# Row vectors through DRAM in 16-byte pieces, read on the chip through strided views

## The chip, the cores and the metric

The kernel runs on one core of one Trainium2 chip, as one launch. The time is the device time of an execution in microseconds (us). All inputs, weights and the output are in DRAM; the profile times are those of one execution.

## The reference

Two transformer blocks over 512 tokens of 1024 numbers, in float32. In the first block a layer that mixes the tokens with a gated MLP (gmlp) is followed by a feed-forward layer (FF), then a layer of sparse attention (nsa) by another FF; the second block is one layer of two kinds of attention side by side. Between the layers stand the operations that matter here; `c` is one vector that steers the whole:

```
def modulate(h, shift, scale):
    return h * (1.0 + scale[:, None, :]) + shift[:, None, :]
...
    mod = c_act @ ada_w[layer] + ada_b[layer]
    sh1, sc1, g1, sh2, sc2, g2 = jnp.split(mod, 6, axis=-1)
    h = modulate(rms_norm(x, norm_g[layer, 0]), sh1, sc1)
...
    x = x + g1[:, None, :] * rms_norm(y, norm_g[layer, 1])
    h = modulate(rms_norm(x, norm_g[layer, 2]), sh2, sc2)
    y = jnp.square(jax.nn.relu(h @ ff_w_in[layer])) @ ff_w_out[layer]
    x = x + g2[:, None, :] * rms_norm(y, norm_g[layer, 3])
```

The second block ends with `x + gate * (mixed @ w_out)`. So each layer needs row vectors of 1024 numbers: a gain G for what it gives out (norm weight times gate), and a scale B and a shift S for the next layer's input.

## The kernel before

The 512 tokens are four chunks (c = 0 to 3) of 128, with tokens in the partitions and the 1024 features along the free axis, in two halves (n = 0, 1) of 512. The stream x stays on the chip (`xs`) until it is set aside in DRAM (`xd`). A float32 product is made of three products of rounded parts, high by high, high by low and low by high; names that end in h and l are such parts (`wh`, `wl` of a weight tile `raw`; `twh`, `twl`, `tah`, `tal` for the last part of an output product), and `fmps` and `acc` are PSUM banks that gather products.

Nothing is issued where it is written: a recorder takes down every operation, plans an order for each engine from a table of its own costs and from the buffers that are free, and then emits the whole (line 615, so nearly every instruction of the profile bears L615 and is found by its tiles). Each engine then goes through its own list in that order and waits where an operand is missing. SP issues all DMAs, in one list. `flex` leaves it to the planner whether DVE or POOL makes a multiplication, `mac` likewise (a product by a scalar per partition, plus a tile). The planner's costs know the number of elements, not their step.

The row vectors come out as columns: `vec` (line 927) takes products of a weight row block with the steering vector on DVE, and leaves a tile [128, 8], where partition p and column k hold element k·128 + p. `col` waits for it and adds the bias. `wide` (line 948) makes rows of it that every partition holds: SP stores the tile to a DRAM scratch row of 1024 numbers, and then reads each half back with a broadcast into a 128x512 tile. This is done for 11 vectors: G1, B2, S2 at the boundary behind gmlp (boundary 1), G2 behind the first FF (2), G3, B4, S4 behind nsa (3), G5, B6, S6 behind the second FF (4), and the gate at the end; a name with w at its end (G1w) is the row. At boundary 2 B and S stay columns (`h_chunk2`). The vectors that `setup` needs at the program's beginning don't go through `wide`.

When a chunk of an output product is done, `boundary` runs three steps for it. `residual` (line 1030): z = acc × G for both halves (DVE), the square sums (ScalarE, named ACT in the profile), 1/rms as `yr`, then x = z·yr + x. `x_rstd`: 1/rms of the new x as `xr`. `h_chunk` (line 1000): hx = x × B (`flex`), hx = hx·xr + S (`mac`), then four transposes of 128x128 for each half on TensorE (PE) into the bank `tp`, from which the next layer's input is split into its parts. `fin` (in `second`) makes the output: fy = acc × gate, fy = fy + x, and the store.

Of the kernel before, what the change touches and what calls it, by code (L numbers as in the profile page):

```python
# [670 lines left out]
class KB:  # L671
# [276 lines left out]
    def wide(self, vec, name):  # L948

        v = self.col(vec)  # L950
        r = self.scratch([1, 1024], name)
        self.sp.dma_start(r.rearrange("o (k p) -> p (o k)", p=128), v)
        t = [self.t2([128, 512], F32, name) for _ in range(2)]
        for n in range(2):
            self.sp.dma_start(t[n], r[:, n * 512:n * 512 + 512].bcast())
        return t


    def x_rstd(self, c):
# [40 lines left out]
    def h_chunk(self, c, r, B, S, hT, keep=None):  # L1000
        if keep is not None:
            return self.h_chunk2(c, r, B, S, hT, keep)
        for n in range(2):
            s = slice(n * 512, n * 512 + 512)
            t = self.t2([128, 512], F32, "hx")
            self.flex("tensor_mul", t, self.xs[c][:, s], B[n])
            self.mac(t, t, r, S[n])
            ps = self.ps("tp")
            for j in range(4):
                self.pe.transpose(ps[:, j * 128:(j + 1) * 128], t[:, j * 128:(j + 1) * 128], self.ident)  # L1010
            cs = slice(c * 128, c * 128 + 128)
            self.split(hT.hi[n][:, :, cs], hT.lo[n][:, :, cs], ps.rearrange("p (j t) -> p j t", j=4))
# [17 lines left out]
    def residual(self, c, banks, G):  # L1030

        ss = self.st(2, "ys")
        z = []
        for n in range(2):
            s = slice(n * 512, n * 512 + 512)
            junk = self.t2([128, 512], F32, "junk")
            self.act.activation(junk, banks[n], AF.Square, accum_out=ss[:, n:n + 1])
            z.append(self.t2([128, 512], F32, "z"))
            self.dve.tensor_mul(z[n], banks[n], G[n])
        r = self.rstd_of(ss, "yr")  # L1040
        for n in range(2):
            s = slice(n * 512, n * 512 + 512)
            x = self.xs[c][:, s]
            self.mac(x, z[n], r, x)
# [631 lines left out]
    def second(self, hT, grow):  # L1676
# [298 lines left out]
        gate = self.wide(grow, "gatew")  # L1975

        def fin(c, banks):
            for n in range(2):
                s = slice(n * 512, n * 512 + 512)
                xt = self.t2([128, 512], F32, "fx")  # L1980
                self.sp.dma_start(xt, self.xd[c][:, s])
                y = self.t2([128, 512], F32, "fy")
                parts = 2 if c == NC - 1 and n == 1 else 1
                for i in range(parts):
                    h = slice(i * 512 // parts, (i + 1) * 512 // parts)
                    self.dve.tensor_mul(y[:, h], banks[n][:, h], gate[n][:, h])
                    self.dve.tensor_add(y[:, h], y[:, h], xt[:, h])
                    self.sp.dma_start(self.out[0, c * 128:(c + 1) * 128, n * 512 + h.start:n * 512 + h.stop], y[:, h])

        self.out_gemm(self.act_f32(mixed), I["w_out_2"][0], KD, fin, CTAIL, split=True)  # L1990

    def build(self):
# [83 lines left out]
```

## Time and profile before

| | |
|---|---|
| median of 3 runs | 1545.78 us (1544.43 to 1546.18) |
| the profiled execution, its own time | 1546.29 us |
| its span | 1544.5 us |
| its mean granted TensorE clock | 0.993 |
| PE busy | 1496.9 us (97%) |
| DVE busy | 1088.8 us (70%) |
| ScalarE busy | 657.2 us (43%) |
| POOL busy | 294.0 us (19%) |
| instructions | 20161 |

Busy time counts an engine's own instructions, not its waiting. In a group of instructions, "idle before" is the time that the engine stood still ahead of them, and behind the arrow stands what ended it. A window is a stretch of the span, in which the busy time of each engine is summed up; a timeline lists one engine's instructions in order of time, with the idle time ahead of one in brackets. In the stages' windows boundary 1 lies at 145 to 205 us, boundary 2 at 495 to 550, boundary 3 at 850 to 905, boundary 4 at 1195 to 1260.

### The profile page before, as it was taken

Reading aid. Unit: us, or ns where it says so; the run is one execution under the profiler, and the core shown is the slowest. Engines: PE = TensorE matmul, PEld = TensorE weight load, DVE = VectorE, ACT = ScalarE, POOL = GpSimd, SP = SyncE. Lnnn points to the kernel's source line nnn. Section 1 sums busy time; section 2 is a strip of 40 time slices with the busy share of each in tenths; the row PEclk is TensorE's granted clock in tenths of the full one; section 3 lists DMA queues with packets and bytes.
Section 4 is the critical chain, followed back from the end, with each engine's and each line's share of the span. In section 5 each row is a group of like instructions: output and inputs, shape, how many; then the busy total and the mean of one; then the engine's idle time right before and its main releaser. Section 6 shows DMA issues by size and latency. Waiting matters only on the chain.

```text
span 1544.5 us, 20161 instructions
## 1 busy us (share of the span) xinstructions
PE 1496.9 (97%) x7410; PEld 1248.8 (81%) x7410; DVE 1088.8 (70%) x2038; ACT 657.2 (43%) x1422; POOL 294.0 (19%) x355
## 2 busy tenths in 40 slices
PE   5999999999999999999999999999999999999998
PEld 4877788888888898778877898888888887878877
DVE  7897866568871679687886864456662669598982
ACT  5523432232120656578774332222120337566870
POOL 2023100000010320465762000000000014132250
PEclk9999999999999999999989999999999999999999
DMA  9874677549620343102124447438411251113112
GB/s 345 263 264 110 213 234 249 171 156 383 271 84 13 133 151 117 52 1 56 28 69 137 135 117 256 134 135 255 154 43 54 96 181 55 55 52 91 50 54 96
DMA packets 151394, 212.97 MB, mean 138 GB/s; under 512 B 49536, under 2 KB 110208, under 8 KB 151296
## 3 DMA queue, kind: packets, MB, share of 16 engines
q1 hardware_dynamic: 151296, 211.69, 42.3%
q8 instruction: 58, 0.95, 0.3%
q14 instruction: 40, 0.33, 0.1%
HBM read 205.33 MB, written 6.34 MB: 137 GB/s over the span
## 4 chain that ended last, share of the span: by engine, by line
PE 76%; DVE 8%; ACT 3%; issue 2%; POOL 1%; DMA 0%; POOLq 0%; DVEq 0%; ACTq 0%
PE acc L615 30%; PE fmps L615 25%; PE qps L615 4%; PE tmc L615 4%; PE po L615 2%; PE sgps L615 2%; DVE wl L615 2%; DVE ptl L615 2%; PE vps L615 1%; PE tmb L615 1%; PE kps L615 1%; PE sB L615 1%; PE tp L615 1%; PE sA L615 1%; PE tA L615 1%
## 5 line engine op out<-in xcount | busy, mean ns | idle before, releaser
L615 DVE TENSOR_TENSOR wl<-raw,wh 128x1024 fp32r<-128x1024 f32 x194 | 240.4, 1242 | 41.3 <-PE fmps L615 18.5
L615 PE MATMUL acc<-wh,ah 128*128 128x512 f32 x432 | 168.9, 391 | 0.0
L615 PE MATMUL acc<-wl,ah 128*128 128x512 f32 x432 | 168.6, 390 | 0.0
L615 DVE CAST wh<-raw 128x1024 fp32r<-128x1024 f32 x118 | 82.9, 703 | 119.9 <-PE fmps L615 93.7
L615 DVE SCALAR_TENSOR_TENSOR raw<-raw,cb 128x1024 f32<-128x1024 f32 x112 | 137.1, 1248 | 11.7 <-DMA raw<-in_kv_ada_w_dram 7.9
L615 PE MATMUL acc<-wh,al 128*128 128x512 f32 x432 | 133.8, 390 | 0.0
L615 ACT ACTIVATE r<-fmps 128x512 f32<-128x512 f32 x64 | 38.2, 597 | 206.9 <-PE fmps L615 206.9
L615 PE MATMUL fmps<-hfh,wl 128*128 128x512 f32 (+1 forms) x288 | 105.5, 366 | 1.1 <-DVE wl L615 1.1
L615 PE MATMUL acc<-twh,tah 128*128 128x512 f32 x272 | 105.1, 392 | 1.1 <-ACT tah L615 1.1
L615 PE MATMUL acc<-twl,tah 128*128 128x512 f32 x272 | 105.4, 393 | 0.6 <-DVE twl L615 0.5
L615 PE MATMUL fmps<-hfl,wh 128*128 128x512 f32 (+1 forms) x288 | 105.2, 366 | 0.2 <-DVE hfl L615 0.2
L615 PE MATMUL fmps<-hf1l,wh 128*128 128x512 f32 (+1 forms) x288 | 105.2, 366 | 0.0
L615 PE MATMUL fmps<-hf1h,wl 128*128 128x512 f32 (+1 forms) x288 | 105.2, 366 | 0.0
L615 PE MATMUL fmps<-hfh,wh 128*128 128x512 f32 (+1 forms) x288 | 105.0, 366 | 0.0
L615 PE MATMUL fmps<-hf1h,wh 128*128 128x512 f32 (+1 forms) x288 | 104.8, 365 | 0.0
L615 ACT CAST ah<-hid 128x512 fp32r<-128x512 f32 x48 | 29.7, 619 | 159.4 <-PE acc L615 159.4
L615 PEld LDWEIGHTS acc<-wh,ah 128*128 128x128 f32 x432 | 81.5, 189 | 16.9
L615 POOL TENSOR_SCALAR tah<-hid 128x512 fp32r<-128x512 f32 x5 | 5.5, 1112 | 470.4 <-DMA raw<-in_ff_w_out_dram 206.5
L615 PEld LDWEIGHTS acc<-wl,ah 128*128 128x128 f32 x432 | 81.4, 188 | 16.8
L615 PEld LDWEIGHTS acc<-wh,al 128*128 128x128 f32 x432 | 81.3, 188 | 16.7
L615 PE MATMUL acc<-twh,tal 128*128 128x512 f32 x272 | 86.8, 394 | 1.1 <-DVE tal L615 1.1
L615 ACT CAST wh<-raw 128x1024 fp32r<-128x1024 f32 x57 | 59.8, 1050 | 55.3 <-PE fmps L615 32.0
(543 smaller groups left out, 3851.4 us busy)
## 6 DMA issues: line engine op xcount, KB each, us to landing
raw<-in_ada_w_dram SPq DMA_DIRECT2D x40, 1024.0 KB, 7.8
raw<-in_ff_w_in_dram SPq DMA_DIRECT2D x32, 1024.0 KB, 9.4
raw<-in_ff_w_out_dram SPq DMA_DIRECT2D x32, 1024.0 KB, 5.0
raw<-in_w_in_dram SPq DMA_DIRECT2D x16, 1024.0 KB, 5.6
raw<-in_w_ada_dram SPq DMA_DIRECT2D x12, 1024.0 KB, 10.8
raw<-in_a_w_in_dram SPq DMA_DIRECT2D x8, 1024.0 KB, 8.9
raw<-in_ada_w_dram SPq DMA_DIRECT2D x16, 512.0 KB, 11.8
raw<-in_kv_ada_w_dram SPq DMA_DIRECT2D x8, 1024.0 KB, 14.2
```

Source lines behind the costliest of these rows:

```text
L615: getattr(real[e], m)(*a, **k)
```

## The change

The store of a row vector writes four neighbouring numbers at a time: of each half n, partition p writes its four columns k behind each other. The half then lies in DRAM, and after the broadcast in the 128x512 tile, in the order p·4 + k, while the feature is k·128 + p. `wide` gives out views of the tiles that read it in the order of the features, [128, 4, 128] with a step of four numbers (16 bytes) in the innermost axis; the users write their other operands in the same three axes (`by4`), which leaves these contiguous. So one operand of each of these multiplications is read with a step, and none is written with one.

```
@@ wide
-        self.sp.dma_start(r.rearrange("o (k p) -> p (o k)", p=128), v)
+        self.sp.dma_start(r.rearrange("o (n p k) -> p (o n) k", n=2, p=128), v.rearrange("p (n k) -> p n k", n=2))
         t = [self.t2([128, 512], F32, name) for _ in range(2)]
         for n in range(2):
             self.sp.dma_start(t[n], r[:, n * 512:n * 512 + 512].bcast())
-        return t
+        return [x.rearrange("q (p k) -> q k p", k=4) for x in t]
+
+    @staticmethod
+    def by4(x):
+
+        return x.rearrange("q (k p) -> q k p", k=4)
@@ h_chunk
-            self.flex("tensor_mul", t, self.xs[c][:, s], B[n])
-            self.mac(t, t, r, S[n])
+            self.flex("tensor_mul", self.by4(t), self.by4(self.xs[c][:, s]), B[n])
+            self.mac(self.by4(t), self.by4(t), r, S[n])
@@ residual
-            self.dve.tensor_mul(z[n], banks[n], G[n])
+            self.dve.tensor_mul(self.by4(z[n]), self.by4(banks[n]), G[n])
@@ fin
-                    self.dve.tensor_mul(y[:, h], banks[n][:, h], gate[n][:, h])
+                    hk = slice(h.start // 128, h.stop // 128)
+                    self.dve.tensor_mul(self.by4(y)[:, hk], self.by4(banks[n])[:, hk], gate[n][:, hk])
```

No instruction changes its place on PE, DVE, ScalarE or POOL. In SP's list, behind the loads for the end of gmlp (`raw<-in_a_w_out_dram`), the stores of G1 and B2 stand where they stood, ahead of a load of the output weight:

```order
 L615 DMA raw<-in_a_w_out_dram 128x2x1024
-L615 DMA G1w<-G_520 128x8x1
-L615 DMA B2w<-B_876 128x8x1
+L615 DMA G1w<-G_520 128x2x4
+L615 DMA B2w<-B_876 128x2x4
 L615 DMA raw<-in_a_w_out_dram 128x2x1024
 L615 DMA G1w<-G1w 128x512 x2
 L615 DMA B2w<-B2w 128x512 x2
```

Only the shape of the two stores is another; the nine stores further on change in the same way. On PE, with the engines that an instruction waits for, the first transposes of a chunk at boundary 1 read:

```order
 L615 MATMUL acc<-twl,tah 128x512
-L615 MATMUL tp<-ident,hx 128x128 [waits DVE_49]
+L615 MATMUL tp<-ident,hx 128x128 [waits DVE_49,Activation_49]
 L615 MATMUL tp<-ident,hx 128x128 x3
 L615 MATMUL acc<-twh,tal 128x512
```

The order is the same, and the first transpose names an event of ScalarE beside that of DVE.

## Rows read from the trace of the kernel before

**Rows 1.** Windows by stage: the four boundaries; us busy by engine, clock, DMA share, GB/s.

```profile
145.00:205.00 60.00, 57.59 (x349) 50.37 (x348) 51.78 (x97) 26.69 (x60) 4.15 (x3) 1.00 0.64 202
...
495.00:550.00 55.00, 55.00 (x261) 45.62 (x260) 33.52 (x86) 32.37 (x83) 16.26 (x25) 1.00 0.46 155
...
850.00:905.00 55.00, 55.00 (x347) 49.64 (x346) 44.46 (x87) 21.90 (x55) 1.72 (x1) 1.00 0.52 173
...
1195.00:1260.00 65.00, 65.00 (x304) 53.73 (x303) 44.99 (x95) 23.54 (x56) 2.94 (x4) 1.00 0.48 164
```

**Rows 2.** DMA issues of the whole program: count, KB each, median us to landing.

```profile
G1w<-G SPq DMA_DIRECT2D x1, 4.0 KB, 10.5
...
xd<-x SPq DMA_DIRECT2D x8, 512.0 KB, 2.6
```

**Rows 3.** Windows around the stores of G1 and B2 and after them.

```profile
116.00:118.00 2.00, 2.00 (x16) 1.81 (x14) 1.26 (x4) 0.60 (x1) 0.00 (x0) 1.00 1.11 5
...
122.00:124.00 2.00, 2.00 (x20) 2.00 (x20) 0.00 (x0) 0.18 (x1) 1.28 (x1) 1.00 0.61 33
...
128.00:144.00 16.00, 13.24 (x53) 9.13 (x52) 15.97 (x16) 6.57 (x9) 10.33 (x6) 1.00 0.51 199
```

**Rows 4.** Timeline of ScalarE: start, us, operation, idle time before it and its releaser.

```profile
123.82 2.00 ACT L615 CAST twh<-raw 128x1024 fp32r<-128x1024 f32 x2 [6.00 <-DMA raw<-in_a_w_out_dram]
```

**Rows 5.** Groups by shape: busy us, mean ns of one, idle before and its releaser.

```profile
L615 DVE SCALAR_TENSOR_TENSOR E<-wsum,lngb,bs 128x128 f32<-128x128 f32 x8 | 2.5, 343 | 0.0
...
L615 DVE SCALAR_TENSOR_TENSOR hx<-hx,xr,S2w 128x512 f32<-128x512 f32 x8 | 5.7, 748 | 1.1 <-DMA S2w<-S2w 1.0
...
L615 DVE SCALAR_TENSOR_TENSOR bl<-R,pos,bh 128x124 fp32r<-128x124 f32 x32 | 13.2, 428 | 1.0 <-ACT bh L615 0.8
...
L615 ACT ACTIVATE PB<-PB,mx 128x128 f32<-128x128 f32 x32 | 12.8, 400 | 5.4 <-DVE mx L615 5.2
...
L615 ACT ACTIVATE PB<-PB,mx 128x384 f32<-128x384 f32 x32 | 19.7, 616 | 4.8 <-DVE mx L615 4.8
...
L615 ACT ACTIVATE bh<-R,pos 128x124 fp32r<-128x124 f32 x32 | 14.3, 509 | 4.2 <-DVE R L615 4.2
...
L615 DVE TENSOR_TENSOR z<-acc,G1w 128x512 f32<-128x512 f32 x8 | 5.4, 685 | 2.4 <-PE acc L615 2.4
...
L615 DVE TENSOR_TENSOR fy<-acc,gatew 128x256 f32<-128x256 f32 x2 | 0.8, 418 | 1.3 <-PE acc L615 1.3
```

**Rows 6.** Timeline of boundary 3, second chunk, DVE then PE.

```profile
863.09 1.29 DVE L615 TENSOR_TENSOR z<-acc,G3w 128x512 f32<-128x512 f32 x2 [0.38 <-PE acc L615]
...
870.54 1.42 DVE L615 SCALAR_TENSOR_TENSOR hx<-hx,xr,S4w 128x512 f32<-128x512 f32 x2
...
872.19 1.29 DVE L615 TENSOR_TENSOR z<-acc,G3w 128x512 f32<-128x512 f32 x2 [0.23 <-PE acc L615]
...
872.67 0.60 PE L615 MATMUL tp<-ident,hx 128*128 128x128 f32 x4
```

**Rows 7.** Timeline of boundary 4, second chunk, DVE then PE.

```profile
1211.68 1.29 DVE L615 TENSOR_TENSOR z<-acc,G5w 128x512 f32<-128x512 f32 x2 [1.86 <-PE acc L615]
...
1217.99 1.41 DVE L615 SCALAR_TENSOR_TENSOR hx<-hx,xr,S6w 128x512 f32<-128x512 f32 x2
...
1220.31 0.60 PE L615 MATMUL tp<-ident,hx 128*128 128x128 f32 x4
```

**Rows 8.** Timeline of boundary 1, last chunk: DVE, POOL, PE.

```profile
177.91 2.36 DVE L615 TENSOR_TENSOR wl<-raw,wh 128x1024 fp32r<-128x1024 f32 x2 [1.38 <-ACT wh L615]
...
185.44 2.04 POOL L615 TENSOR_TENSOR hx<-x,B2w 128x512 f32<-128x512 f32 x1 [1.43 <-DVE x L615]
...
190.34 1.32 PE L615 MATMUL tp<-ident,hx 128*128 128x128 f32 x8 [1.06 <-DVE hx L615]
```

**Rows 9.** Timeline of boundary 2, last chunk, ScalarE then PE.

```profile
545.48 0.72 ACT L615 ACTIVATE hx<-x,xr 128x512 f32<-128x512 f32 x1
...
546.50 1.03 PE L615 MATMUL tp<-ident,hx 128*128 128x128 f32 x8
```

## The prediction

> **What bounds the kernel now.** I read the windows by stage first. The four boundaries, where one layer's result is multiplied by a gain, added to the stream, normed and turned into the next layer's input, are all TensorE time: PE is busy 57.59 of 60, 55.00 of 55, 55.00 of 55 and 65.00 of 65 us [rows 1]. The program's own order decides what happens there: each engine runs a fixed list, and PE's list holds the transposes of the new input (tile tp) between other products. So VectorE (DVE) may be late by the slack between its last multiplication of a chunk and that chunk's tp; every us beyond is a us of idle PE, and nothing later gives it back, since PE has no spare time afterwards. DVE is itself full at boundary 3 (44.46 of 55, and nearly without gaps from the first z on) and lighter at boundaries 2 and 4 [rows 1].
>
> Second I read the DMA issues and the windows around the first stores. A row vector's store, 4 KB, takes 10.5 us to land, while 512 KB of x land in 2.6 us [rows 2]. While the stores of G1 and B2 are under way, the DMA engines are full and move 5 GB/s; DVE has 0.00 us of work in 122 to 124 [rows 3], because the load of w_out that queues behind those pieces comes late: ScalarE waits 6.00 us for it [rows 4]. In the following products PE has 13.24 us of work in 16, and DVE 15.97 [rows 3].
>
> **What the change removes.** Each of the 11 stores goes from 1024 pieces of 4 bytes to 256 of 16. Nothing in the trace has 16-byte pieces; the landing lies between 2.6 and 10.5 us [rows 2]. I take 2.6 plus a quarter of the other 7.9, about 4.6 us: the pieces, not the bytes, fill the engines. The w_out load then comes some 5 us sooner, DVE can use its empty stretch, and the dense stretch after it starts earlier. Its PE idle time, 16 − 13.24 = 2.76 us, is the most that can be won; the least is 0, if DVE, full there, stays the limit. I take 2.0, since the idle DVE time ahead is about as long as the loss. The stores' other effect is S2: DVE waits 1.0 us for the S2 row at boundary 1 [rows 5]; that wait goes. The eight later stores I cost at nothing: DVE's multiplications by G wait for PE's acc [rows 5, 6, 7], so those rows are there by then.
>
> **What the change adds.** DVE's and POOL's order stays the same, but one operand of 89 multiplications is now read with a step of 16 bytes: 32 z (8 at each boundary), 24 hx by B and 24 hx by S (8 of each at boundaries 1, 3 and 4), 9 fy at the end. The trace has just one reading with a large step, the blocks of R (step 64 bytes). On DVE, 128 contiguous elements take 343 ns and 512 take 748: 1.05 ns each on a fixed 208. The strided bl takes 428 for 124: (428 − 208)/124 = 1.77 ns each. On ScalarE, 128 and 384 contiguous elements take 400 and 616: 0.84 ns each on a fixed 292; the strided bh takes 509: 1.75 ns each [rows 5]. Two engines of different pace fall to the same 1.76 ns, so it is the reading that limits them. If a step of 16 bytes does the same, an operation on 512 elements grows by 512 × 0.72 = **0.37 us**. The bounds are 0 (16 bytes is near enough to contiguous) and a second full pass, 512 × 1.05 = 0.54. I take 0.37, the only strided rows there are.
>
> The Trainium skill ("SBUF — State Buffer", section on Door 1, the DMA port swizzle) says that SBUF has lines of 16 bytes, and that an access that crosses to a new line pays a penalty. A step of 16 bytes opens a new line with each element, as 64 bytes does; so the rule speaks against this change, and the bl and bh rows agree with it as far as they reach. The page gives no price.
>
> Now place by place, with 0.37 us.
>
> Boundary 1: PE waits 1.06 us for DVE's hx at the last chunk already [rows 8], so there DVE's lateness goes straight to PE. Of 24 operations one is on POOL (its 2.04 us end at 187.5, while DVE's last hx will come after 190) and the first three z lie in 2.4 us of waiting for PE [rows 5]: 20 × 0.37 = 7.4. Off it go the S2 wait, 1.0, and the 1.38 us that DVE waits for ScalarE's wh [rows 8], which it will no longer reach in time to wait: **+5.0**.
>
> Boundary 2: only z is strided, 2 × 0.37 = 0.74 a chunk. At the last chunk ScalarE's hx ends at 546.20 and tp starts at 546.50 [rows 9]: 0.74 − 0.30 = 0.44, the other chunks have more slack: **+0.5**.
>
> Boundary 3: DVE has no room. 24 × 0.37 = 8.9, less the gaps of 0.38 and 0.23 ahead of z, less one slack: the hx pair that starts at 870.54 ends at 871.96, its second tp starts at 872.67, 0.71 [rows 6]: **+7.5**. The same pattern stands at all four chunks.
>
> Boundary 4: DVE waits 1.86 us for PE before a chunk's z [rows 7], so each chunk starts afresh. Its six operations make 2.2 us; the hx pair ends at 1219.40, and the second tp is at 1220.31 [rows 7]: 2.2 − 0.9 = 1.3, three times, and 1.5 for the last chunk, which has hardly any slack but a wait of DVE ahead: **+5.4**.
>
> End: the last two fy work on 256 elements, 418 ns each [rows 5], and the output waits for them: 2 × 0.19, **+0.4**.
>
> Some of PE's transposes also wait for a ScalarE event now. I cost this at nothing: the square roots on ScalarE that it may mean lie ahead of the DVE operation that the same transpose waits for.
>
> The sum is 5.0 + 0.5 + 7.5 + 5.4 + 0.4 − 2.0 = +16.8 us. The profiled execution took 1546.29 us (span 1544.5), 0.5 above the median of the runs, 1545.78. So 1546.3 + 16.8 = 1563.1 by the profile, and **1562.5** as a median. With 0.25 us for an operation the same terms make +8.4, with 0.45 about +23: this case's own range is 1554 to 1569.
>
> **Rivals.**
> (1) *The 16-byte step is free.* For it: the only strided rows have a step four times as long and blocks of 31 elements, so they may not speak for this one. Against it: two engines show the limit. Then z and hx cost what they did and only the stores count: −2.0, between 0 and −2.76. The S2 wait adds nothing, because DVE would then wait longer for wh at 177.91 [rows 8]. The time is 1543 to 1546, likeliest 1543.8. It decides below some 0.13 us for an operation: there the slacks (0.71 and 0.9) and DVE's waits hide nearly all, and what is left is the gain of the stores. The same section of the Trainium skill goes on that one can stride freely as far as 4 fp32, which read literally is this case; no row of the trace shows it.
> (2) *A second pass.* Each strided operand costs the whole pace once more, 0.54 us. For it: crossing a line with every element may cost more than bl, whose second operand is short. Against it: bl and bh share one pace. By the same terms boundary 1 makes 8.4, boundary 3 11.6, boundary 4 9.6, the rest 2.2: +29.8 after the stores, about 1575.5.
> (3) *The stores don't get shorter*, because the 16 bytes still travel as four pieces. Nothing is won: +18.8, some 1564.5, and landings of 10 us would show it.
>
> **Chances and range.** A measurement of this kernel can tell about 0.2%, 3.1 us, from no change: below 1542.7 is faster, above 1548.9 slower. The forecast has 0.66, (1) 0.22, (2) 0.08, (3) 0.04. Slower by over 0.2%: 0.66 + 0.08 + 0.04, less 0.01 for a small step cost in the forecast, 0.77. The free step gives 0.17 within 0.2% and 0.05 faster, as its gain would have to pass 3.1 us; with the 0.01, 0.18 within 0.2%. The range runs from 1543.5, inside the free case, to 1572; what is left out is about half of (1) and most of (2), under 0.2. Cases of one sign hold most of the chance; their own range is above.
>
> **What the next profile would show.** Right: z about 1.05 us in place of 0.685, hx by S about 1.12 in place of 0.748, store landings of 4 to 5 us, PE idle ahead of tp (released by DVE hx) at boundaries 1, 3 and 4 with 5, 7.5 and 5.4 us, at boundary 2 hardly any; ScalarE's 6.00 us wait shorter, and PE above 15 us in 128 to 144. The forecast is wrong if z stays near 0.69 us (then rival 1), if z is at 1.2 (rival 2), or if DVE is late as reckoned and PE doesn't wait, which would mean that the slack ahead of tp is larger than the rows show.

## The result: slower by 1.4%, and the profile after

| | before | after |
|---|---|---|
| median of 4 runs each, on one chip | 1545.94 us | 1567.59 us (1563.17 to 1569.89) |
| ratio, 95% interval | | 1.0139 [1.0115, 1.0162] |
| the profiled execution's span | 1544.5 us | 1566.2 us |

The change costs 21.7 us, as a median and in the two spans alike. The forecast was 1562.5, in a range of 1543.5 to 1572. First the page of the changed kernel, its busy time by engine:

```profile
span 1566.2 us, 20168 instructions
...
PE 1501.3 (96%) x7410; PEld 1251.5 (80%) x7410; DVE 1123.5 (72%) x2038; ACT 657.4 (42%) x1422; POOL 292.2 (19%) x355
```

DVE has 34.7 us more work (1088.8 before), and its instructions are as many as before. The groups by shape say which became longer; after the bar stand the busy us, the mean ns of one, and the idle time before with its releaser:

```profile
L615 DVE SCALAR_TENSOR_TENSOR bl<-R,pos,bh 128x124 fp32r<-128x124 f32 x32 | 13.3, 429 | 1.0 <-ACT bh L615 0.8
L615 DVE SCALAR_TENSOR_TENSOR hx<-hx,xr,S4w 128x512 f32<-128x512 f32 x8 | 9.6, 1240 | 0.1
L615 DVE SCALAR_TENSOR_TENSOR hx<-hx,xr,S2w 128x512 f32<-128x512 f32 x8 | 9.5, 1231 | 0.1
L615 DVE SCALAR_TENSOR_TENSOR hx<-hx,xr,S6w 128x512 f32<-128x512 f32 x8 | 8.7, 1135 | 0.1
L615 DVE TENSOR_TENSOR z<-acc,G1w 128x512 f32<-128x512 f32 x8 | 8.4, 1068 | 2.0 <-PE acc L615 2.0
L615 DVE TENSOR_TENSOR hx<-x,B4w 128x512 f32<-128x512 f32 x8 | 8.4, 1086 | 0.0
...
L615 DVE TENSOR_TENSOR fy<-acc,gatew 128x256 f32<-128x256 f32 x2 | 1.1, 596 | 0.7 <-PE acc L615 0.7
```

Two of these groups as they were in the kernel before:

```profile
L615 DVE SCALAR_TENSOR_TENSOR hx<-hx,xr,S6w 128x512 f32<-128x512 f32 x8 | 5.7, 748 | 0.1
L615 DVE TENSOR_TENSOR hx<-x,B4w 128x512 f32<-128x512 f32 x8 | 5.1, 684 | 0.0
```

So hx by S6 went from 748 to 1135 ns, +0.387 us, and hx by B4 from 684 to 1086, +0.402; against [rows 5], z went from 685 to 1068, +0.383, and fy on half the elements from 418 to 596, +0.178. That is 0.70 to 0.79 ns an element, where bl, the same at 429, had let 0.72 be expected. The means of 1231 and 1240 for hx by S2 and S4 hide something else, below.

What PE makes of it is in its waits and its timeline (start, us, operation, idle time before it and the releaser):

```profile
PE tp L615 <- DVE hx L615: 17.0, 22, 2.1
...
160.88 0.63 PE L615 MATMUL tp<-ident,hx 128*128 128x128 f32 x4 [0.75 <-DVE hx L615]
168.86 0.63 PE L615 MATMUL tp<-ident,hx 128*128 128x128 f32 x4 [1.25 <-DVE hx L615]
194.39 0.66 PE L615 MATMUL tp<-ident,hx 128*128 128x128 f32 x4 [2.07 <-DVE hx L615]
882.72 0.63 PE L615 MATMUL tp<-ident,hx 128*128 128x128 f32 x4 [1.36 <-DVE hx L615]
1224.51 0.63 PE L615 MATMUL tp<-ident,hx 128*128 128x128 f32 x4 [0.89 <-DVE hx L615]
1252.86 0.63 PE L615 MATMUL tp<-ident,hx 128*128 128x128 f32 x4 [1.80 <-DVE hx L615]
```

The first line is the sum of PE's waits for hx ahead of tp: us in all, how often, the longest. In the kernel before it reads:

```profile
PE tp L615 <- DVE hx L615: 1.1, 1, 1.1
```

So PE waited once, for 1.1 us; now it waits 22 times, 17.0 us in all. The transposes at 872.67 [rows 6] had slack; the same ones now start at 883.76, 7.7 us late from the places ahead and 3.4 from this boundary's first two chunks.

The stores got shorter, and ScalarE's wait for w_out [rows 4] is gone. The DMA issues (count, KB, us to landing), then ScalarE's timeline, then the window that lies over the products behind gmlp, with busy us by engine in the order PE, PEld, DVE, ACT, POOL:

```profile
raw<-in_a_w_out_dram SPq DMA_DIRECT2D x4, 1024.0 KB, 5.6
...
G1w<-G SPq DMA_DIRECT2D x1, 4.0 KB, 4.6
B2w<-B SPq DMA_DIRECT2D x1, 4.0 KB, 4.5
S2w<-S SPq DMA_DIRECT2D x1, 4.0 KB, 1.5
```

```profile
118.39 1.99 ACT L615 CAST twh<-raw 128x1024 fp32r<-128x1024 f32 x2
```

```profile
128.00:144.00 16.00, 14.84 (x65) 11.38 (x65) 15.96 (x18) 4.62 (x7) 5.32 (x4) 1.00 0.39 131
```

The weight's cast stands at 118.39 without a wait, against 123.82, and PE has 14.84 us of work in those 16 us against 13.24 [rows 3].

Since PE's list is the same in both kernels, the start of the same PE instruction in the two traces gives its lateness, and the growth of the lateness across a place is what the place lost. Worked out in this way from the profiled executions, each against the trace of before (us):

| place | forecast | after | stores alone | step alone | gmlp rows only | gains alone | casts off POOL |
|---|---|---|---|---|---|---|---|
| behind gmlp (110 to 144) | −2.0 | −2.4 | −2.3 | −0.4 | −2.3 | −2.3 | −2.3 |
| boundary 1 (144 to 205) | +5.0 | +6.9 | −0.1 | +6.6 | +5.8 | +0.6 | +5.5 |
| boundary 2 (495 to 550) | +0.5 | +0.6 | 0.0 | +0.6 | 0.0 | +0.6 | +0.6 |
| boundary 3 (848 to 905) | +7.5 | +8.0 | 0.0 | +8.0 | 0.0 | +2.2 | +7.2 |
| boundary 4 (1195 to 1260) | +5.4 | +6.6 | −0.1 | +6.6 | −0.1 | +0.7 | +6.2 |

The other columns are the experiments. Between the places the lateness stays: from 205 to 495 and from 905 to 1195 it is the same to 0.1 us. The changed kernel's sum here is 19.7; 0.4 at the end, 0.7 ahead of the first place, and +1.9 (550 to 848) and −1.0 (1260 to 1515) in stages where no row vector is multiplied make the rest. In those stages the granted clock falls for some us at places that vary: between 800 and 850 it is 0.80 in the changed kernel and 0.83 in the kernel before, which is half speed for some 20 us against 17. Experiment 4, which loses nothing at the boundaries, gains 1.5 us in 1260 to 1515, so a gain there is no slack that takes up a lateness.

### The profile page after: what moved, and what is told of

It is laid out like the page before. It is cut to its first block, busy times and chain, and to the rows that moved or that the text cites. A ratio compares the mean times of both kernels' runs of the same rounds, so it can differ in the third digit from the quotient of the medians.

```text
span 1566.2 us, 20168 instructions
## 1 busy us (share of the span) xinstructions
PE 1501.3 (96%) x7410; PEld 1251.5 (80%) x7410; DVE 1123.5 (72%) x2038; ACT 657.4 (42%) x1422; POOL 292.2 (19%) x355
## 4 chain that ended last, share of the span: by engine, by line
PE 69%; DVE 14%; ACT 4%; issue 3%; POOL 1%; POOLq 0%; DVEq 0%; ACTq 0%
PE acc L615 25%; PE fmps L615 24%; PE tmc L615 4%; PE qps L615 4%; DVE hx L615 3%; PE po L615 3%; DVE wl L615 2%; PE sgps L615 2%; DVE ptl L615 1%; DVE z L615 1%; PE kps L615 1%; DVE x L615 1%; PE sB L615 1%; PE sA L615 1%; PE tmb L615 1%
## 6 DMA issues: line engine op xcount, KB each, us to landing
raw<-in_kv_ada_w_dram SPq DMA_DIRECT2D x8, 1024.0 KB, 10.5
```

## The experiments

All but the last issue the instructions of the changed kernel in the same order; only the pieces and views differ, and in experiment 5 the columns that the sums go to. Each was timed beside the kernel before on the same chip.

**1. The stores alone.** The rows go out in 16-byte pieces and are read contiguously.

```
-        return [x.rearrange("q (p k) -> q k p", k=4) for x in t]
+        return [x.rearrange("q (k p) -> q k p", k=4) for x in t]
```

> The stores go in 16-byte pieces as in the changed kernel, but the rows are read contiguously, so the features of each row are taken in the wrong order; the work is the same. My theory, that the whole loss is in the strided reading and the stores are a gain: z at 0.68 us, hx by S at 0.75, PE's waits for DVE hx ahead of tp back at about 1 us in all (17.0 in the changed kernel), the 2.4 us won in the stretch behind gmlp kept, hence about 1543.5 us, 1542 to 1545. The rival, that the transfers which now start earlier collide with others and carry part of the loss: 1548 or more, with z at 0.68.

Measured: 1542.63 us against 1545.13 for the kernel before, ratio 0.9985 [0.9976, 0.9994]. z is back at 0.685 and hx by S4 at 0.748 us; the boundaries lose nothing. So the stores are worth some 2.4 us (2.3 by the place, 2.5 by the medians), and no transfer that starts earlier takes part in the loss. The rows are still read through the three axes of `by4` here, only without a step: the axes alone cost nothing.

```profile
L615 DVE SCALAR_TENSOR_TENSOR hx<-hx,xr,S4w 128x512 f32<-128x512 f32 x8 | 5.7, 748 | 0.1
...
L615 DVE TENSOR_TENSOR z<-acc,G3w 128x512 f32<-128x512 f32 x8 | 5.2, 685 | 12.5 <-PE acc L615 12.5
```

**2. The step alone.** The stores of before, read through the strided views.

```
-        self.sp.dma_start(r.rearrange("o (n p k) -> p (o n) k", n=2, p=128), v.rearrange("p (n k) -> p n k", n=2))
+        self.sp.dma_start(r.rearrange("o (k p) -> p (o k)", p=128), v)
```

> The stores are those of before (1024 pieces of 4 bytes), the rows are read through the strided views, so the features are in the wrong order; the work is the same. My theory: z at 1.07, hx by S at 1.12 to 1.24, landings of 10 us, ScalarE's wait of 6 us for w_out back, the gain of 2.4 us gone: about 1570 us, and the waits of S2 hidden behind nothing, so up to 1571. The rival, that earlier loads carry part of the loss: clearly below 1567.

Measured: 1565.96 us, ratio 1.0129 [1.0113, 1.0146], 20.8 us over the kernel before. By the total this is a miss: 1570 was expected, and below 1567 was what the rival asked for. The places decide it: the loss at each boundary is that of the changed kernel (6.6, 0.6, 8.0, 6.6), and the gain behind gmlp is gone (−0.4). The stages between 550 and 848 and behind 1260 took 1.9 us less here than before and 0.9 more in the changed kernel, and no row is multiplied in either. I had added two totals of which each carries some us of its own.

**3. The rows of boundary 1 only.** G1, B2 and S2 go the new way, the other eight the old.

```
+        if name in ("G1w", "B2w", "S2w"):
             self.sp.dma_start(r.rearrange("o (n p k) -> p (o n) k", n=2, p=128), v.rearrange("p (n k) -> p n k", n=2))
+        else:
+            self.sp.dma_start(r.rearrange("o (k p) -> p (o k)", p=128), v)
...
+        pat = "q (p k) -> q k p" if name in ("G1w", "B2w", "S2w") else "q (k p) -> q k p"
+        return [x.rearrange(pat, k=4) for x in t]
```

> Only G1, B2 and S2, the rows of boundary 1, are stored in 16-byte pieces and read with a step; the other eight go the old way and are read contiguously. My theory, that each place's loss stands alone and nothing later gives it back: -2.4 behind gmlp and +6.9 at boundary 1, +4.5 us, 1550.5 (1549 to 1552). If the 3.4 us at half clock that follow PE's last stall at boundary 1 are chance, 1548.8. The rival, that the slack of later stages takes up a lateness: 1546 or less.

Measured: 1550.98 us against 1545.13, ratio 1.0036 [1.0024, 1.0048], +5.9, inside the range. In the trace boundary 1 loses 5.8 and the others nothing; the lateness is the same, 4.0 us, from 205 to 495, and boundaries 2 to 4 take up none of it. The places stand alone. The hit of the median is in part luck: the traced execution is the fastest of the six, 1548.18, its clock doesn't fall behind PE's last stall, and its two places add up to 3.5, near the 1548.8 that was named for that case. What the other executions lost beyond it, no trace shows.

**4. A step of 8 bytes.** Pieces of two numbers, and views with a step of two numbers.

```
-        ... r.rearrange("o (n p k) -> p (o n) k", n=2, p=128), v.rearrange("p (n k) -> p n k", n=2))
+        ... r.rearrange("o (n p k) -> p (o n) k", n=4, p=128), v.rearrange("p (n k) -> p n k", n=4))
-        return [x.rearrange("q (p k) -> q k p", k=4) for x in t]
+        return [x.rearrange("q (m p k) -> q k m p", m=2, k=2) for x in t]
-        return x.rearrange("q (k p) -> q k p", k=4)
+        return x.rearrange("q (k m p) -> q k m p", k=2, m=2)
```

> Pieces of 8 bytes (512 for a row) and a step of 8 bytes in the views; columns 1 and 2 of each half are exchanged, the work is the same. The step alone decides whether the price belongs to any step or to one of 16 bytes and more. By the first theory, that every element apart from its neighbour costs, z stays at 1.07 us and the time at 1567 to 1569. By the second, that two elements in one stretch of 16 bytes are enough, z is back at 0.68 us, and with landings of about 5 to 7 us the time is 1543 to 1546. The Trainium skill (SBUF, State Buffer, Door 1) speaks for the second: it asks for two hits in a line of 16 bytes.

Measured: 1541.62 us against 1545.13, ratio 0.9984 [0.9974, 0.9993], 1.4 below the expected range. Groups and DMA issues:

```profile
L615 DVE SCALAR_TENSOR_TENSOR hx<-hx,xr,S4w 128x512 f32<-128x512 f32 x8 | 5.7, 749 | 0.1
...
L615 DVE TENSOR_TENSOR z<-acc,G1w 128x512 f32<-128x512 f32 x8 | 5.4, 686 | 2.9 <-PE acc L615 2.9
```

```profile
G1w<-G SPq DMA_DIRECT2D x1, 4.0 KB, 5.7
...
S2w<-S SPq DMA_DIRECT2D x1, 4.0 KB, 3.0
```

A step of 8 bytes costs nothing: 749 and 686 ns, what contiguous rows cost. The store still lands in 5.7 us in place of 10.5, and the gain behind gmlp is 2.4 us, as with 16-byte pieces. So the price begins between 8 and 16 bytes (12 was not tried). The Trainium skill ("SBUF — State Buffer", section on Door 1, the DMA port swizzle) asks for two hits in each line of 16 bytes, and these rows agree with that; its next sentence, read as leave to step by 4 fp32, does not agree with the z of 1068 ns.

**5. The step of 8 bytes as a whole kernel.** The same, with the columns of a vector gathered in the order in which pairs go out (`at`), and bias and norm weight read through views that fit:

```
+        vec.at = [i % 2 * 4 + i // 2 if name in self.WIDE else i for i in range(KD)]
...
+        self.sp.dma_start(r.rearrange("o (n p k) -> p (o n) k", n=4, p=128), v.rearrange("p (n k) -> p n k", n=4))
+        r = r.rearrange("o (j h q) -> o h j q", j=2, h=2)
+            self.sp.dma_start(t[n].rearrange("q (j s) -> q j s", j=2), r[:, n].bcast())
```

> The step of 8 bytes as a whole kernel: the sums of a vector are gathered in the order in which pairs of columns go to DRAM, the bias and the norm weight are read to fit through views of 4x2, so no instruction is added, and each row is read back as two pieces of 256. My theory: as with the columns exchanged, z at 0.69 us, the gain behind gmlp kept (2.2 to 2.4 us), 3.0 us less than the kernel before, 1541.5 to 1543.5. The rival: reading a row back in two pieces, or the small additions through views, costs on the path and takes the gain away, 1545 or more.

Measured: 1543.78 us against 1546.11, ratio 0.9987 [0.9972, 1.0002]. Its trace shows what was expected: z 0.684 to 0.685, hx by S 0.748, the boundaries at most 0.5 better or 0.2 worse, 2.9 us won behind gmlp. The median is 0.3 us above the range that was expected and below the rival's 1545. It is 1.5% ahead of the changed kernel; the 2.3 us against the kernel before have the sign of experiments 1 and 4, but the interval of this run alone takes in no difference.

**6. Only the gains strided.** G1, G2, G3, G5 and the gate have the step of 16 bytes, B and S are read contiguously:

```
+        pat = "q (p k) -> q k p" if name[0] in "Gg" else "q (k p) -> q k p"
+        return [x.rearrange(pat, k=4) for x in t]
```

> Stores as in the changed kernel; only the five rows that are multiplied into the outputs (G1, G2, G3, G5, gate) are read with a step of 16 bytes, 41 of 89 multiplications; the B and S rows are read contiguously, so their features are in the wrong order. My theory, that a boundary loses only what passes its slack: boundary 1 none or 0.5 (5 z of 0.38 against 2.4 us of waits), boundary 2 0.6, boundary 3 3.0 - 0.6 - 0.7 = 1.7, boundary 4 0.4 (two z of 0.38 stay under the slack of 0.9 but at the last chunk), end 0.4, behind gmlp -2.4: about +0.8 us beside the kernel before, 1545 to 1547. The rival, that the loss goes with the number of strided operations (41 of 89 of some 22 us, less 2.4): +7.7 us, 1553.

Measured: 1549.34 us against 1546.11, ratio 1.0016 [1.0004, 1.0028], +3.2: a miss of the range (0.8 was forecast), far from the rival's 7.7. By places boundary 1 lost 0.6, boundary 2 0.6, boundary 3 2.2, boundary 4 0.7, and with the end and the gain behind gmlp that is +2.2; the traced execution, 1545.78, is the fastest of the twelve, so the median's last us is not placed. The 41 operations cost 4.2 us in the boundaries, where all 89 cost 22. At boundary 4 the first transposes of the first three chunks wait for nothing:

```profile
1207.87 0.63 PE L615 MATMUL tp<-ident,hx 128*128 128x128 f32 x4
...
1219.69 0.62 PE L615 MATMUL tp<-ident,hx 128*128 128x128 f32 x4
...
1232.46 0.63 PE L615 MATMUL tp<-ident,hx 128*128 128x128 f32 x4
1233.91 0.63 PE L615 MATMUL tp<-ident,hx 128*128 128x128 f32 x4 [0.59 <-DVE hx L615]
```

Two z of +0.38 lie under the slack of 0.9; six operations do not. The one wait, 0.59 ahead of the third chunk's second four, is not the gains'. DVE's and POOL's timelines just before it:

```profile
1231.56 2.20 DVE L615 SCALAR_TENSOR_TENSOR hx<-hx,xr,S6w 128x512 f32<-128x512 f32 x2
...
1231.90 1.33 POOL L615 TENSOR_SCALAR wh<-raw 128x1024 fp32r<-128x1024 f32 x1 [70.09 <-DMA raw<-in_w_in_dram]
```

The pair of hx by S6, read contiguously here, takes 2.20 us in place of 1.41, beside a cast of POOL. The lateness at boundary 4 is 0.0 us up to the transposes at 1232.46, 0.8 at those at 1233.91 and 0.7 at the end, so this pair makes the whole of it. The six z that come before it cost nothing, nor do the last two. At boundary 1 the 0.6 is the gains': an rt beside a cast takes 1.04 us in place of 0.21, but in the kernel before a cast held up as much there (experiment 7). The loss is what passes the slack, and not a price for each operation.

**7. Three casts off POOL.** In the changed kernel some rows of boundaries 1, 3 and 4 are longer than the step explains. DVE's and POOL's timelines:

```profile
177.56 2.98 DVE L615 SCALAR_TENSOR_TENSOR hx<-hx,xr,S2w 128x512 f32<-128x512 f32 x2
...
177.91 1.71 POOL L615 TENSOR_SCALAR wh<-raw 128x1024 fp32r<-128x1024 f32 x1 [42.31 <-DMA raw<-in_ff_w_in_dram]
...
891.92 2.96 DVE L615 SCALAR_TENSOR_TENSOR hx<-hx,xr,S4w 128x512 f32<-128x512 f32 x2
...
892.00 1.95 POOL L615 TENSOR_SCALAR wh<-raw 128x1024 fp32r<-128x1024 f32 x1 [52.07 <-PE acc L615]
...
1250.31 1.06 DVE L615 SCALAR_TENSOR_TENSOR rt<-xr,hv 128x1 f32<-128x1 f32 x1 [0.51 <-ACT xr L615]
...
1250.31 1.04 POOL L615 TENSOR_SCALAR wh<-raw 128x1024 fp32r<-128x1024 f32 x1 [72.91 <-DMA raw<-in_w_in_dram]
```

The pairs of hx take 2.98 and 2.96 us where the others take 2.2, and an operation on one column takes 1.06, as long as POOL's cast beside it. Before, these casts met other operations. The edit, where the operations are emitted (its five lines move that place from line 615 to 620):

```
+            if e == "pool" and m == "tensor_scalar" and a[0].buf.name == "wh":
+                if casts in (3, 7, 8):
+                    e, m, a, k = "act", "copy", a[:2], {}
+                casts += 1
```

> The changed kernel with three casts wh<-raw (one at each of boundaries 1, 3 and 4) made by ScalarE where POOL makes them; the rest of each list is as it was. In the changed kernel POOL's cast lies beside a strided hx by S at boundaries 1 and 3 (1.92 us in place of 1.14) and beside a small rt operation at boundary 4 (1.06 us in place of 0.22). My theory, that DVE's operation is held up by POOL's cast and that this is part of the loss: these three rows go to 1.14, 1.14 and 0.22, the losses at boundaries 1, 3 and 4 fall by about 0.8 each, and the time by 2.4, to 19 us above the kernel before, 1565. The rival, that these rows are long for another reason or lie off PE's path: rows as long as in the changed kernel, or short with 21 to 22 us still lost. A cast that makes ScalarE late would show as PE waiting for ScalarE ahead of acc or tp.

Measured: 1562.83 us against 1544.93, ratio 1.0121 [1.0105, 1.0138], +17.9. The groups:

```profile
L620 DVE SCALAR_TENSOR_TENSOR hx<-hx,xr,S2w 128x512 f32<-128x512 f32 x8 | 8.8, 1138 | 0.1
L620 DVE SCALAR_TENSOR_TENSOR hx<-hx,xr,S4w 128x512 f32<-128x512 f32 x8 | 8.8, 1134 | 0.1
...
L620 DVE SCALAR_TENSOR_TENSOR rt<-xr,hv 128x1 f32<-128x1 f32 x16 | 3.5, 216 | 4.0 <-ACT xr L620 4.0
```

All hx by S are at 1.13 us, the long rt is gone (the mean of rt was 270 ns in the changed kernel), and PE's wait for hx falls from 17.0 to 14.9 us. Boundaries 1, 3 and 4 lose 1.3, 0.7 and 0.4 us less, 2.5 in all: close to the sum that was expected, but not 0.8 each, and at boundary 1 it is in part luck.

At boundary 3 experiment 2 has the long hx and no drop of the clock, and loses the same 8.0 as the changed kernel, whose clock is at 0.55 in 895 to 897; so the 0.7 are the cast's. At boundary 4 the third chunk loses 0.8 us less, which is the long rt, and the last chunk 0.4 more than in the changed kernel.

At boundary 1 POOL makes a second cast, which stays on POOL in this run, and it holds up another operation in most runs. DVE, then POOL, in the kernel before; DVE in the changed kernel; DVE, then POOL, in this run:

```profile
183.03 2.18 DVE L615 SCALAR_TENSOR_TENSOR x<-z,yr,x 128x512 f32<-128x512 f32 x2
...
182.96 1.05 POOL L615 TENSOR_SCALAR wh<-raw 128x1024 fp32r<-128x1024 f32 x1 [5.02 <-DMA raw<-in_ff_w_in_dram]
...
184.85 0.53 DVE L615 SCALAR_TENSOR_TENSOR hv<-ys,hv 128x1 f32<-128x1 f32 x1
...
184.32 0.70 DVE L620 SCALAR_TENSOR_TENSOR hv<-ys,hv 128x1 f32<-128x1 f32 x1
...
183.96 1.05 POOL L620 TENSOR_SCALAR wh<-raw 128x1024 fp32r<-128x1024 f32 x1 [48.18 <-DMA raw<-in_ff_w_in_dram]
```

The pair of x takes 1.41 us without a cast beside it, and this hv 0.16. So the kernel before lost 0.77 us to a cast that the strided kernels don't lose, and they lose others. DVE has no idle time from the long hx to the last one, so each goes straight to PE. The table adds this up; the clock's part is the lateness that grows behind PE's last four transposes, where the clock falls in two runs and stays at full in two (below).

| boundary 1, us | after | step alone | gmlp rows only | casts off POOL |
|---|---|---|---|---|
| lost | 6.86 | 6.60 | 5.77 | 5.52 |
| casts: hx + hv, less the 0.77 of before | 0.78 + 0.38 − 0.77 | 0.78 + 0.12 − 0.77 | 0.79 + 0 − 0.77 | 0 + 0.54 − 0.77 |
| clock | 0.73 | 0.76 | 0 | 0 |
| left for the step | 5.7 | 5.7 | 5.7 | 5.7 |

So this run's gain of 1.3 at boundary 1 is 0.6 of casts and 0.7 of clock, and in the changed kernel the casts are worth 0.4 + 0.7 + 0.4 = 1.5 us against the kernel before. My theory holds for the three rows and for 1.7 of its 2.4 us. The time, +17.9 for an expected +19, is again lower by what the stages without rows did.

## Why the prediction was right, point by point

**The price of the step.** 0.37 us forecast from bl and bh, 0.38 to 0.40 measured for z and hx. That a step of 64 bytes priced one of 16 held on DVE, and experiment 4 adds where the price starts. That the reading limits both engines stays an inference: no run reads a row with a step on ScalarE. Rival 1, a free step, falls with the z of 1068 ns, rival 2 (0.54 us) as well. Rival 2's "rest 2.2" is 1.3 by its own terms (0.78 at boundary 2 and 0.54 at the end), which moves its 1575.5 to 1574.6 and decides nothing.

**The stores.** Landing 4.6 us forecast, 4.6 measured for G1, and down to 1.5 for S2. The agreement is in part luck: the sum took 2.6 us as the least, and S2 lies below it. Behind gmlp −2.0 was forecast and −2.4 measured, with PE at 14.84 us of work in 128 to 144, just short of the 15 that was named as a sign; experiment 1 shows that this gain stands by itself. The later stores were costed at nothing: from 205 to 495 and at boundaries 2 to 4 experiment 1 moves no place by more than 0.1 us. Rival 3 falls with the landings.

**Slack first, then a loss that stays.** Boundary 2 +0.5 forecast, +0.6 measured; boundary 3 +7.5 and +8.0; the end +0.4 and +0.4. Experiments 3 and 6 show both halves of the argument: a place's loss isn't given back, and what stays below the slack costs nearly nothing.

**Two terms were too small.** Boundary 1 was put at +5.0 and lost 6.9, boundary 4 at +5.4 and lost 6.6. In both the step "so many operations × 0.37, less the waits" took DVE's other operations as they were. It left out that a DVE that runs late meets POOL's casts at other places of its list (0.4 us at boundary 1, 0.7 at boundary 3, 0.4 at boundary 4), and that PE's long wait at boundary 1 can be followed by a slower clock (0.7).

What is left is the price itself. At boundary 4 the first two chunks of the changed kernel lose 1.44 and 1.46 us, where 1.3 was forecast: two z, two hx by B and two by S at the measured 0.38, 0.40 and 0.39 make 2.34, less the slack of 0.91. At boundary 1 the step is left with 5.7 against 5.0. The same 20 operations at the measured prices make 7.8 in place of 7.4, and one DVE product (`raw<-raw,cb`) takes 2.33 us in place of 2.07 while POOL's own strided hx takes 2.30 in place of 2.04; 5.0 + 0.4 + 0.3 is an estimate that meets the 5.7, and no run tried it by itself.

At boundary 3 the forecast of 7.5 and the 8.0 agree better than they should: without the cast 7.2 are lost. The total was 5 us short: 3.1 by the two terms, 1.6 by what the start and the stages without rows happened to do (0.7 + 0.9), half a us at boundary 3, less the 0.4 more that was won behind gmlp.

**The added ScalarE event** on PE's transposes cost nothing: PE's waits ahead of tp name hx, and experiment 1, which has that event too, loses nothing.

## What to carry to other kernels

Price a strided operand by the nearest strided row that the trace holds, and look at whether two elements still lie side by side: a step of 8 bytes was free here, one of 16 made each DVE operation 0.38 to 0.40 us longer on 512 elements. A transfer that is slow because of its small pieces need not be made as fast as can be: pieces of 8 bytes won as much as pieces of 16, since what was left was hidden. And where PE takes an engine's result in a fixed order, compare the added durations with the slack ahead of that result, chunk by chunk: what stays below it costs nearly nothing, and what passes it is paid and kept. A list that runs late also meets another engine's work at other places, so look there before laying a difference on the change itself.

## What was not expected of the hardware

**Some DVE operations stand still while POOL casts a wide tile.** A DVE operation on a 128x1 column took 1.06 us beside a POOL cast of 128x1024 that took 1.04, and 0.22 in the run that moved the cast; hx by S took 1.92 beside such a cast and 1.14 without. Contiguous operations are held as well: the hx by S6 of experiment 6 and the x of the kernel before. POOL's own cast grew in turn, to 1.71 and 1.95 us, where hx was already running when it began. Not every operation is held: the changed kernel's z at 183.83, which reads a PSUM bank, took 1.10 us across the start of the cast at 184.34, and 1.07 in the mean.

**The clock after a stall.** Windows of the changed kernel around PE's last transposes at boundary 1; the number behind the five engines is the granted clock:

```profile
192.00:194.00 2.00, 0.32 (x3) 0.11 (x1) 1.93 (x4) 0.00 (x0) 0.00 (x0) 1.00 1.09 362
194.00:196.00 2.00, 1.20 (x7) 0.97 (x8) 2.00 (x3) 0.58 (x1) 0.00 (x0) 0.87 1.04 404
196.00:198.00 2.00, 2.00 (x11) 1.94 (x9) 1.91 (x4) 0.59 (x1) 0.00 (x0) 0.50 1.06 357
198.00:200.00 2.00, 2.00 (x15) 2.00 (x15) 2.00 (x3) 0.00 (x0) 0.00 (x0) 0.78 1.09 375
```

PE worked 1.5 us of the four up to 196, and the clock is at half, 1.2 GHz, in the window behind. So a stall can cost more than its own length: behind the start of its last four transposes boundary 1 lost another 0.73 and 0.76 us in the two runs that show this drop (the changed kernel and the step alone), and nothing in the two that don't (gmlp rows only, casts off POOL). The run with the casts moved has the same stall:

```profile
192.00:194.00 2.00, 0.01 (x1) 0.01 (x1) 1.93 (x5) 0.00 (x0) 0.00 (x0) 1.00 1.11 365
194.00:196.00 2.00, 1.59 (x11) 1.22 (x11) 2.00 (x2) 0.84 (x2) 0.00 (x0) 1.00 1.02 399
```

There the clock stays at full. What decides between the two stays open; it may be one reason why the changed kernel's runs lie 6.7 us apart, which was not tried.
